# Low parts of weights on VectorE in two halves, bias tiles kept beside the keys, transpositions four steps behind the scores

## The chip, the cores and the metric

The kernel runs on one core of a Trainium2 chip. Five engines of that core work in parallel, each through its own queue in order: TensorE (PE in the profile, with its weight loads as PEld), VectorE (DVE), ScalarE (ACT), GpSimd (POOL) and SyncE (SP), which here issues nearly all DMAs. An instruction waits at the head of its queue until what it needs is there, and everything behind it on that engine waits too.

The metric is the device time of one execution in microseconds (us), as the median of three runs. The profile is of one further execution.

## The reference, cut to what matters

One layer of a streaming encoder. The tokens (1024 of a new stream, 64 of a running one) are normalized and projected to ten groups of columns; two kinds of attention follow, then gates, two projections, a merge and an output projection. The parts around the change:

```python
def stick_breaking(q, k, v, q_pos, k_pos):                # branch A ("sb"), 8 heads of 64
    z = jnp.einsum("bqhd,bkhd->bhqk", q, k).astype(jnp.float32) * ATTN_SCALE
    causal = k_pos[None, :] < q_pos[:, None]
    log_beta = jax.nn.log_sigmoid(z)
    log_keep = jnp.where(causal, jax.nn.log_sigmoid(-z), 0.0)
    suffix = lax.cumsum(log_keep, axis=3, reverse=True) - log_keep
    w = jnp.where(causal, jnp.exp(log_beta + suffix), 0.0)
    return jnp.einsum("bhqk,bkhd->bqhd", w.astype(v.dtype), v)

def band_attention(q, k, v, q_pos, k_pos, rel_bias):      # branch B ("cb"), 8 heads of 64
    s = jnp.einsum("...qhd,...khd->...hqk", q, k).astype(jnp.float32) * ATTN_SCALE
    rel = jnp.clip(q_pos[..., :, None] - k_pos[..., None, :], -REL_CLIP, REL_CLIP) + REL_CLIP
    bias = jnp.moveaxis(rel_bias[:, rel], 0, -3).astype(jnp.float32)
    s = jnp.where(mask, s + bias, NEG_INF)
    p = jax.nn.softmax(s, axis=-1).astype(v.dtype)
    return jnp.einsum("...hqk,...khd->...qhd", p, v)

...
    b_sb = (o_sb.reshape(lead + (WIDTH_SB,)) * jax.nn.silu(z_sb)) @ w_proj_sb
    b_cb = (o_cb.reshape(lead + (WIDTH_CB,)) * jax.nn.silu(z_cb)) @ w_proj_cb
    h = jax.nn.sigmoid(g_sb) * b_sb + jax.nn.sigmoid(g_cb) * b_cb
    return x + h @ w_out
```

## The kernel before, in words

**Precision.** Products of weights and activations run on operands of type fp32r. Each operand is split into a high part (a copy to that type on ScalarE) and a low part (what the copy lost, a subtraction), and three products are added: high by high, high by low, low by high. In class `Weights`, `hi` is the copy (L115) and `lo` the subtraction (L122), on GpSimd unless an engine is named; `split` issues both.

**Stages.** The input projection (L464, then L634) takes the first half. The attention loop at the end of the listing below (`for i in range(len(seq) + LAG)`) runs from about 512 to 872 us of the span. The projection of the "cb" branch (L925) and the output projection (L1419) follow.

**The attention loop.** `seq` lists 136 steps: branch "sb" first, then "cb"; in each, four pairs `p` of heads; in each pair the 64 running tokens (`t == 8`, both heads in one step), then eight blocks `t` of 128 queries for each head `hd`. A step of "sb" is as wide as `(t + 1) * 128` keys, one of "cb" at most 640. Iteration `i` issues, in this order:

- `mid(i - 2, 1)`: for "cb", reciprocal and scaling on VectorE (L1060, L1061); `mid(i - 1, 0)`: for "sb", the scan that forms the suffix products and the multiplication (L1057, L1058, VectorE), for "cb" the exponential (L1054, ScalarE)
- `tr(i - LAG)`: transpositions of the finished weights `be` on TensorE (L1088) in groups of up to four blocks into `pt`, of which there are two buffers in PSUM, and copies from there to `wT` on ScalarE (L1095)
- half of the step's filler (`fill`)
- `qk(i)`: scores `z` on TensorE (L1034, three buffers); for "sb" two sigmoids on ScalarE (L1036 into `kp`, L1037 into `be`) and, ahead of these, a one-column memset of `kp` on GpSimd (L1023); for "cb" one custom VectorE instruction that adds the bias tile and keeps a running minimum (L1039)
- loads: `load_z`, and in `prefetch` the next queries, keys, values and bias tiles, each at its own `t`
- stores that were put off (`flush`), the rest of the filler, and, after each second block of queries, the products with the values `av` (L1123), whose result VectorE multiplies by the gate (L1127)

`be` has four buffers, `kp` three.

**The filler.** `fill(n)` pulls `n` matmuls out of the generator `run_fill`: eight units of the input projection that were left over (72 matmuls each, L781), and then the "sb" output projection `proj_sb` (24 matmuls for each of 12 pieces, L881). They give TensorE work while VectorE and ScalarE finish a step. The eighth unit may not begin before step ("cb", 0, 1); until then what is asked of `fill` is owed. How much a step gets is in proportion to its width, out of `n_sb` for all "sb" steps and `n_cb = 72 + FP` for all "cb" steps. Whenever a unit or a piece `ci == 1` begins, the generator also splits the weights of the next one; inside `proj_sb`'s first stretch and the eighth unit, `og_step` splits the attention outputs (`og_hi` on ScalarE, `og_lo` on GpSimd for even pairs and VectorE for odd).

**The bias tiles.** `load_bias(p)` issues four DMAs and four memsets. The tiles live in pool `ay`, which is opened when "cb" begins, in the memory that the "sb" pool `axs` (with `kp`) has just left; the first pair's tiles are therefore loaded in the first iteration of "cb" (L1206), the later ones in the pair before, at `t == 4` (L1152).

```python
    FP = 180
    n_sb = 72 * (len(units) - 3)
    n_cb = 72 + FP
...
    LAG = 3
...
            if (b, p, t) == ("cb", 0, 8):
                sbx.close()
                yst = ExitStack()
                late["y"] = yst.enter_context(tc.tile_pool(name="ay", bufs=2))
                load_bias(0)
            qk(i)
```

## Time and profile before

| what | value |
|---|---|
| median of three runs | 1027.22 us (1025.51 to 1031.51) |
| the profiled execution | 1026.61 us, of which the span 1024.8 us |
| VectorE busy over the span | 630.6 us (62%) |
| ScalarE busy | 498.2 us (49%) |
| GpSimd busy | 340.7 us (33%) |
| granted TensorE clock, mean | 0.99 |

The page counts a matmul as busy until its modelled end, and matmuls overlap, so a share of 95% or more on PE means only that it hardly waited; the idle time in front of an instruction, and what ended it, says where it did. In groups of instructions, the number behind the second bar is the engine's idle time just before them, followed by what ended it. In the timeline a row is start, length, engine, line, operation, output <- inputs, shapes, count, and in brackets the idle time before it.

### The profile page before, as it was taken

Reading aid. Unit: us, or ns where it says so; the run is one execution under the profiler, and the core shown is the slowest. Engines: PE = TensorE matmul, PEld = TensorE weight load, DVE = VectorE, ACT = ScalarE, POOL = GpSimd, SP = SyncE. Lnnn points to the kernel's source line nnn. Section 1 sums busy time; section 2 is a strip of 40 time slices with the busy share of each in tenths; the row PEclk is TensorE's granted clock in tenths of the full one; section 3 lists DMA queues with packets and bytes.
Section 4 is the critical chain, followed back from the end, with each engine's and each line's share of the span. In section 5 each row is a group of like instructions: output and inputs, shape, how many; then the busy total and the mean of one; then the engine's idle time right before and its main releaser. Section 6 shows DMA issues by size and latency. Waiting matters only on the chain.

```text
span 1024.8 us, 20492 instructions
## 1 busy us (share of the span) xinstructions
PE 973.2 (95%) x7568; PEld 922.4 (90%) x7568; DVE 630.6 (62%) x1181; ACT 498.2 (49%) x1149; POOL 340.7 (33%) x356
## 2 busy tenths in 40 slices
PE   6999999999999999999989999996989988999998
PEld 5999999998989999999978978885877777999998
DVE  5466673984534555422078879893776765389735
ACT  6544442444343333333267867773765654366320
POOL 3377662124444444542210011012110100377451
PEclk9999999999999999999999999998999998999999
DMA  7636468435555333332686657646898871773542
GB/s 244 205 124 208 164 236 290 127 106 160 165 170 153 96 95 125 111 97 81 183 223 177 162 136 183 157 127 177 226 249 244 229 219 45 230 237 102 191 133 87
DMA packets 177412, 171.04 MB, mean 167 GB/s; under 512 B 35040, under 2 KB 163168, under 8 KB 177184
## 3 DMA queue, kind: packets, MB, share of 16 engines
q1 hardware_dynamic: 168592, 161.41, 53.3%
q10 hardware_dynamic: 8720, 8.33, 2.5%
q8 instruction: 60, 0.98, 0.4%
q14 instruction: 40, 0.33, 0.1%
HBM read 110.96 MB, written 58.72 MB: 166 GB/s over the span
## 4 chain that ended last, share of the span: by engine, by line
PE 77%; DMA 7%; DVE 5%; SPq 4%; ACT 3%; issue 2%; POOL 1%; DVEq 0%; ACTq 0%; POOLq 0%
PE b L634 23%; PE acc L464 19%; PE b L1419 7%; PE o L1123 7%; PE acc L781 6%; PE pt L1088 5%; PE z L1034 5%; PE b L925 2%; SPq L51 2%; PE acc L881 1%; DVE be L1039 1%; DVE be L1061 1%; DMA d_ksbT<-hl 1%; DMA wo<-in_w_out_dram 1%; PE pk L349 1%
## 5 line engine op out<-in xcount | busy, mean ns | idle before, releaser
L1088 PE MATMUL pt<-ident,be 128*128 128x128 f32 (+1 forms) x568 | 88.7, 281 | 29.4 <-ACT wT L1095 12.2
L1095 ACT ACTIVATE wT<-pt 128x512 f32<-128x512 f32 (+3 forms) x200 | 87.5, 474 | 58.8 <-PE pt L1088 58.4
L122 POOL TENSOR_TENSOR wlo<-wraw,whi 128x1024 fp32r<-128x1024 f32 x22 | 53.5, 2433 | 176.9 <-ACT whi L115 131.9
L1088 PEld LDWEIGHTS pt<-ident,be 128*128 128x128 f32 (+1 forms) x568 | 65.6, 142 | 44.0 <-issue 17.9
L1057 DVE TENSOR_TENSOR_SCAN kp<-kp,imp 128x128 f32<-128x128 f32 (+7 forms) x64 | 88.0, 1375 | 0.0
L1034 PE MATMUL z<-ks,sq 128*128 128x320 f32 (+5 forms) x384 | 85.0, 330 | 0.0
L464 PE MATMUL acc<-whi,xa 128*128 128x256 f32 x256 | 74.2, 292 | 0.0
L1123 PE MATMUL o<-wT,vp 128*64 128x256 f32 (+1 forms) x608 | 70.7, 369 | 1.0 <-ACT wT L1095 1.0
L464 PE MATMUL acc<-wlox,xm 128*128 128x256 f32 x256 | 70.8, 278 | 0.0
L464 PE MATMUL acc<-whi,xm 128*128 128x256 f32 x256 | 70.8, 278 | 0.0
L464 PE MATMUL acc<-wlo,xa 128*128 128x256 f32 x256 | 70.7, 278 | 0.0
L464 PE MATMUL acc<-whix,xb 128*128 128x256 f32 x256 | 70.6, 278 | 0.0
L464 PE MATMUL acc<-whix,xm 128*128 128x256 f32 x256 | 70.6, 278 | 0.0
L1054 ACT ACTIVATE be<-be,sm 128x640 f32<-128x640 f32 (+5 forms) x68 | 47.6, 701 | 46.4 <-DVE sm L1039 41.5
L1123 PEld LDWEIGHTS o<-wT,vp 128*64 128x64 f32 x608 | 44.6, 142 | 26.5 <-issue 7.0
L1034 PEld LDWEIGHTS z<-ks,sq 128*128 128x128 f32 x384 | 66.0, 191 | 0.9
L781 PE MATMUL acc<-xm,whi 128*128 128x384 f32 (+1 forms) x192 | 65.7, 342 | 0.0
L1058 DVE TENSOR_TENSOR be<-be,kp 128x128 f32<-128x128 f32 (+8 forms) x68 | 57.3, 843 | 9.1
L642 DVE TENSOR_TENSOR u<-b,s 128x256 f32<-128x256 f32 (+1 forms) x48 | 21.0, 439 | 63.6 <-PE b L634 63.3
L1036 ACT ACTIVATE kp<-z 128x384 f32<-128x384 f32 (+6 forms) x104 | 52.1, 501 | 8.2 <-PE z L1034 6.6
L1037 ACT ACTIVATE be<-z 128x384 f32<-128x384 f32 (+6 forms) x104 | 52.6, 505 | 0.0
L1127 DVE TENSOR_TENSOR zt<-o,zt 128x256 f32<-128x256 f32 (+1 forms) x40 | 15.3, 383 | 54.1 <-PE o L1123 47.4
(297 smaller groups left out, 3133.0 us busy)
## 6 DMA issues: line engine op xcount, KB each, us to landing
wraw<-in_w_in_dram SPq DMA_DIRECT2D x32, 512.0 KB, 4.5
wrawx<-in_w_in_dram SPq DMA_DIRECT2D x16, 512.0 KB, 4.5
sq<-d_qsbT SPq DMA_DIRECT2D x32, 192.0 KB, 3.6
sq<-d_qcbT SPq DMA_DIRECT2D x32, 192.0 KB, 4.1
gt<-d_gsb SPq DMA_DIRECT2D x30, 192.0 KB, 3.3
xt<-in_x_prompt_dram SPq DMA_DIRECT2D x8, 512.0 KB, 5.0
d_kcbT<-hl SPq DMA_DIRECT2D x8, 512.0 KB, 4.5
d_qcbT<-hl SPq DMA_DIRECT2D x8, 512.0 KB, 5.7
```

What stands on the lines that cost most here:

```text
L122: (eng or G).tensor_tensor(out=l, in0=raw, in1=h[:].bitcast(F32), op=OP.subtract)
L464: TE.matmul(ps, x, w, start=m == 0, stop=m == len(steps) - 1)
L634: TE.matmul(ps[:, :m], w[:, hl_, k], right[s](x)[:, k, a:b], start=s < 3 and k == 0 and e == 0, stop=k == 3 and e == 2, skip_group_check=s ...
L781: TE.matmul(ps[:, :b - a], w[:, k], xk(x, k)[:, a:b], start=k == 0 and n == 0, stop=k == KT - 1 and n == 2)
L1034: TE.matmul(z[:r, :m], s[:, c, q0:q0 + r], ks[:, h, o + x:o + y], start=e == 0, stop=e == len(parts) - 1)
L1037: A.activation(be[:r, x:y], z[:r, :m], AF.Sigmoid, scale=0.125)
L1057: V.tensor_tensor_scan(kp[:r, n - 1::-1], kp[:r, n - 1::-1], im[:, ::-1], 0.0, op0=OP.mult, op1=OP.add)
L1058: V.tensor_tensor(out=be[:r, :n], in0=be[:r, :n], in1=kp[:r, 1:n + 1], op=OP.mult)
L1088: TE.transpose(pt[:kr, x, :r], be[:r, kb * 128:kb * 128 + kr], ident[:r, :r])
L1095: A.activation(w[:, sl:sl + m, q0:q0 + r], pt[:, :m, :r], AF.Copy)
L1123: TE.matmul(o[hd * 64:hd * 64 + 64, c0:c1], vv[:kr, kb, hd * 64:hd * 64 + 64], (wT[b, p, j, hd, s // 4][:kr, s % 4, c0:c1] if j < 4 else w ...
L1419: TE.matmul(ps[:, t], left[s](xs_, k)[:, ts_], wt_[:, k], start=s < 3 and t == k == e == 0, stop=k == 3 and e == 2, skip_group_check=s > 2 ...
```

## The change

Five edits, all in the attention and what it draws on.

1. A new generator `halves` in `Weights`. The filler calls it four times, six matmuls of a unit (three of a projection piece) apart: the first call issues the high copy on ScalarE, the third and the fourth each half of the low subtraction, now on VectorE. The two splits that were issued at `ci == 1` use it.
2. `og_lo` of the "sb" branch runs on VectorE for all pairs.
3. The bias tiles are allocated in pool `am`, beside the queries and values; the first "cb" pair's are loaded in the last "sb" pair at `t == 4`.
4. `LAG` is 4: `tr(i - 4)` and what hangs on it.
5. `FP` is 132, 48 less, and each of the four iterations behind the last step asks for 12 filler matmuls, where it asked for none.

```diff
+        def halves(self, key):
+            self.hi(key)
+            yield
+            raw, pool, shape, extra = self.raw.pop(key)
+            h = self.sp[key][0]
+            l = pool.tile(shape, F32R, name="wlo" + extra, bufs=2)
+            m = shape[1] // 2
+            for c in (slice(0, m), slice(m, 2 * m)):
+                yield
+                V.tensor_tensor(out=l[:, c], in0=raw[:, c], in1=h[:, c].bitcast(F32), op=OP.subtract)
+            self.sp[key] = (h, l)
...
+    cut = [None]
...
-                            W.split(("u", j + 1) if j + 1 < len(units) else ("p", 0))
+                            cut[0] = W.halves(("u", j + 1) if j + 1 < len(units) else ("p", 0))
+                        if ci == 1 and n == 0 and k % 2 == 0:
+                            next(cut[0], None)
...
-        (V if p % 2 else G).tensor_tensor(out=og(b, 1, p)[:, a:e], in0=ot[:, :e - a],
+        (G if b == "cb" and p % 2 == 0 else V).tensor_tensor(out=og(b, 1, p)[:, a:e], in0=ot[:, :e - a],
...
-                W.split(("p", i + 1))
+                cut[0] = W.halves(("p", i + 1))
...
+                        if ci == 1 and uu == 0 and m == 0:
+                            next(cut[0], None)
...
-        if b == "cb" and t == 4:
+        if (b == "cb" or p == NPAIR - 1) and t == 4:
             load_bias(np_)
...
-        bt = late["y"].tile([128, 576], F32, name="bias8", bufs=1)
+        bt = am.tile([128, 576], F32, name="bias8", bufs=1)
...
-            bt = late["y"].tile([128, 640], F32, name="bias", bufs=4)
+            bt = am.tile([128, 640], F32, name="bias", bufs=4)
...
-    FP = 180
+    FP = 132
...
-    LAG = 3
+    LAG = 4
...
+        else:
+            m = 12
...
-                load_bias(0)
```

The places where it moves instructions, as each engine's queue has them. First TensorE where "sb" ends and "cb" begins: `kss` are the first "cb" scores, `be` the weights that are transposed. Before:

```order
L1088 MATMUL pt_9045<-ident_129,be_8924 128x128 x4
L1088 MATMUL pt_9052<-ident_129,be_8924 128x128 x3
L1034 MATMUL z_9074<-kss_8684,sqs_6521 128x288 x4
L1034 MATMUL z_9080<-kss_8684,sqs_6521 128x288 x4
L1088 MATMUL pt_9096<-ident_129,be_8962 128x128 x4
L1088 MATMUL pt_9102<-ident_129,be_8962 128x128 x4
L1034 MATMUL z_9110<-ks_8638,sq0_8897 128x128 x2
L1088 MATMUL pt_9122<-ident_129,be_9021 128x128 x4
L1088 MATMUL pt_9128<-ident_129,be_9021 128x128 x4
L1034 MATMUL z_9136<-ks_8638,sq0_8897 128x128 x2
```

And now:

```order
L1105 MATMUL pt_9049<-ident_129,be_8889 128x128 x4
L1105 MATMUL pt_9056<-ident_129,be_8889 128x128 x3
L1051 MATMUL z_9067<-kss_8686,sqs_6521 128x288 x4
L1051 MATMUL z_9073<-kss_8686,sqs_6521 128x288 x4
L1105 MATMUL pt_9091<-ident_129,be_8932 128x128 x4
L1105 MATMUL pt_9098<-ident_129,be_8932 128x128 x3
L1051 MATMUL z_9105<-ks_8639,sq0_8902 128x128 x2
L1105 MATMUL pt_9117<-ident_129,be_8970 128x128 x4
L1105 MATMUL pt_9123<-ident_129,be_8970 128x128 x4
L1051 MATMUL z_9131<-ks_8639,sq0_8902 128x128 x2
L1105 MATMUL pt_9138<-ident_129,be_9012 128x128 x4
L1105 MATMUL pt_9144<-ident_129,be_9012 128x128 x4
```

The last "sb" step (eight blocks, `be_9021` before and `be_9012` now) is transposed one score later, and one "sb" step more stands behind the first "cb" scores.

Second, SyncE around the last "sb" pair, where `kss` are the keys of the first "cb" step and `bias` the tiles of the first "cb" pair. Before, the bias loads stand alone at the end:

```order
L734 DMA vp<-d_cbv 128x8x128
L735 DMA vs<-in_cache_cb_v_dram 128x4x128
L736 DMA vs<-d_cbv 64x128
L694 DMA d_osb_112<-zt 128x256
L1159 DMA bias_9061<-d_rb_117 64x576
L1159 DMA bias_9061<-d_rb_118 64x576
L1163 DMA bias<-d_rb_117 128x640
L1163 DMA bias<-d_rb_118 128x640
L1101 DMA zt<-d_zcb_89 128x64
```

Now they stand between the key loads and the weights of the projection:

```order
L51 DMA kss<-d_ccbT_81 64x512 x4
L51 DMA kss<-d_kcbT_73 64x64 x4
L706 DMA d_gcb_106<-sg 128x288
L706 DMA d_gcb_106<-sg 128x32
L1176 DMA bias_8748<-d_rb_117 64x576
L1176 DMA bias_8748<-d_rb_118 64x576
L1180 DMA bias<-d_rb_117 128x640
L1180 DMA bias<-d_rb_118 128x640
L706 DMA d_osb_112<-zt 128x256
L109 DMA wraw<-in_w_proj_sb_dram 128x4x256
```

They come some twenty queue entries earlier. On GpSimd their four memsets follow: they stand ahead of the `kp` memsets of the last seven "sb" steps.

Third, VectorE in the third "sb" pair, where one split's two halves now stand among scans (`SCALAR_TENSOR_TENSOR`) and multiplications; before there was none of them here, and one whole `wlo` of 128x1024 on GpSimd:

```order
L138 TENSOR_TENSOR wlo_7817<-wraw_7356,whi_7797 128x512
L1074 SCALAR_TENSOR_TENSOR kp_7870<-kp_7870,ims_6517 128x576
L1075 TENSOR_TENSOR be_7869<-be_7869,kp_7870 128x576
L1074 SCALAR_TENSOR_TENSOR kp_7913<-kp_7913,imp_6514 128x128
L1075 TENSOR_TENSOR be_7912<-be_7912,kp_7913 128x128
L138 TENSOR_TENSOR wlo_7817<-wraw_7356,whi_7797 128x512
```

The loop issues 12 such pairs of halves in all: two ahead of the first scan, eight between scans and "cb" steps, one behind the last step, one after the loop.

## Prediction

> **What bounds the kernel now.** I first read the busy shares, then the groups of instructions with their idle time, then windows of the attention, and last the timeline around each wait.

> ```profile
> PE 973.2 (95%) x7568; PEld 922.4 (90%) x7568; DVE 630.6 (62%) x1181; ACT 498.2 (49%) x1149; POOL 340.7 (33%) x356
> ```

> TensorE is busy for 973 of 1024.8 us, so a change can gain only where TensorE stands, or where it runs slowly. Among the groups one stands out by its idle time, the transpositions in the attention:

> ```profile
> L1088 PE MATMUL pt<-ident,be 128*128 128x128 f32 (+1 forms) x568 | 88.7, 281 | 29.4 <-ACT wT L1095 12.2 <-DVE be L1061 10.9 <-DVE be L1058 5.3
> ```

> TensorE stood 29.4 us in front of them: 12.2 for ScalarE's copies that empty `pt`, 16.2 (10.9 + 5.3) for VectorE to finish `be`. That is most of what TensorE waits for at all, and the change aims at nothing else. How near the other engines are shows in windows: a "sb" pair, two "cb" pairs, the tail of the loop, and the matmuls behind it (behind the times: length, then busy time of PE, PEld, DVE, ACT, POOL, then granted clock).

> ```profile
> 599.00:644.00 45.00, 43.33 (x326) 37.90 (x326) 39.41 (x41) 33.51 (x85) 4.22 (x19) 1.00 0.58 149
> ...
> 743.00:783.00 40.00, 36.66 (x283) 30.98 (x282) 30.61 (x102) 24.48 (x64) 4.04 (x6) 1.00 0.86 237
> 783.00:823.00 40.00, 36.14 (x276) 30.09 (x275) 27.25 (x96) 22.82 (x62) 2.97 (x5) 1.00 0.87 241
> ...
> 863.00:872.00 9.00, 7.04 (x46) 4.91 (x46) 2.91 (x9) 3.87 (x10) 0.00 (x0) 0.81 0.04 15
> 872.00:893.00 21.00, 19.69 (x121) 18.88 (x118) 8.03 (x14) 6.39 (x12) 7.50 (x6) 1.00 0.76 233
> ```

> VectorE is second everywhere: 39.4 of 45 us in "sb", 27 to 31 of 40 in "cb". There is some room for more on it, not much.

> **Low parts off GpSimd.** The GpSimd subtractions of the attention that come just ahead of a TensorE wait, and two VectorE multiplications of the same shape, 128x512:

> ```profile
> 526.51 2.73 POOL L122 TENSOR_TENSOR wlo<-wraw,whi 128x1024 fp32r<-128x1024 f32 x1 [4.73 <-ACT whi L115]
> ...
> 712.41 2.38 POOL L122 TENSOR_TENSOR wlo<-wraw,whi 128x1024 fp32r<-128x1024 f32 x1 [15.32 <-issue]
> 754.33 2.35 POOL L122 TENSOR_TENSOR wlo<-wraw,whi 128x1024 fp32r<-128x1024 f32 x1 [8.06 <-ACT whi L115]
> 799.16 2.38 POOL L122 TENSOR_TENSOR wlo<-wraw,whi 128x1024 fp32r<-128x1024 f32 x1 [22.32 <-ACT whi L115]
> 843.61 2.36 POOL L122 TENSOR_TENSOR wlo<-wraw,whi 128x1024 fp32r<-128x1024 f32 x1 [28.77 <-ACT whi L115]
> ```
> ```profile
> 527.20 2.59 DVE L1058 TENSOR_TENSOR be<-be,kp 128x512 f32<-128x512 f32 x1
> ...
> 661.95 0.69 DVE L1058 TENSOR_TENSOR be<-be,kp 128x512 f32<-128x512 f32 x1
> ```

> The one that starts inside a GpSimd subtraction takes 2.59 us, the other 0.69: VectorE lost 1.9 us until GpSimd was done (526.51 + 2.73 = 529.24; the multiplication ends at 529.79). TensorE then waits:

> ```profile
> 529.93 0.76 PE L1088 MATMUL pt<-ident,be 128*128 128x128 f32 x4 [1.85 <-DVE be L1058]
> ...
> 716.35 0.41 PE L1088 MATMUL pt<-ident,be 128*128 128x128 f32 x2 [2.46 <-DVE be L1061]
> ...
> 756.97 0.41 PE L1088 MATMUL pt<-ident,be 128*128 128x128 f32 x2 [2.23 <-DVE be L1061]
> ...
> 801.91 0.52 PE L1088 MATMUL pt<-ident,be 128*128 128x128 f32 x3 [1.27 <-DVE be L1061]
> ...
> 846.40 0.63 PE L1088 MATMUL pt<-ident,be 128*128 128x128 f32 x4 [1.85 <-DVE be L1061]
> ```

> Each stands two to four us behind the start of one of those five subtractions; together 9.66 us. With none left on GpSimd in the loop I take back **9.0**, between 5 (the new halves delay some of the same weights) and 9.7.

> [...]

> Two of these waits are followed by a stretch of half clock:

> ```profile
> 530.30:533.70 3.40, 3.40 (x15) 3.30 (x14) 3.13 (x4) 2.02 (x5) 0.10 (x1) 0.50 0.44 104
> 694.10:700.90 6.80, 3.27 (x16) 2.78 (x18) 2.18 (x10) 3.87 (x10) 0.58 (x4) 0.50 1.03 281
> 847.80:851.10 3.30, 3.30 (x15) 2.62 (x15) 1.66 (x6) 1.98 (x5) 0.00 (x0) 0.50 0.00 0
> 868.30:871.60 3.30, 3.30 (x15) 1.88 (x17) 0.00 (x0) 0.57 (x2) 0.00 (x0) 0.50 0.00 0
> ```

> TensorE was busy throughout 530.3 to 533.7 and 847.8 to 851.1 at clock 0.50, so half of 6.7 us is lost; with the waits gone I take **3.3** back (0 to 3.3).

> What VectorE pays: of twelve pairs of halves, eight stand between scans and "cb" steps, 16 x 0.69 = 11.0 us; six `og_lo` of at most 128x384 come from GpSimd, below 6 x 0.69 = 4.1. In return nine GpSimd subtractions no longer stretch it, by up to 1.9 us each, 17 in all. Net about nothing on VectorE, which has 5.6 us of room in the "sb" pair and more in "cb"; on TensorE's path I put it at 0 (bounds: 2 us less, 15 us more if nothing comes back). Behind a half in VectorE's queue stand the next scan or bias addition; they wait at most for ScalarE's high copy, issued 12 filler matmuls earlier.

> **Four steps behind.** A transposition now waits for weights that are one step older. Apart from the five waits above, 16.2 - 9.66 = 6.5 us of waiting on VectorE are left. The wait goes where VectorE is late by less than a step, and shrinks where it is later; I take **4.5** (bounds 0 and 6.5). `be` has four buffers, so its writer follows the transpositions of the same iteration; the scores stand behind these on TensorE anyway, and the write waits for the scores, so nothing is added. What may come late next is `pt`: two buffers, emptied by copies that stand behind an exponential on ScalarE. Of the 12.2 us there, all but those at the boundary and in the tail (below) stay in the sum.

> **Bias tiles early.** The boundary between the branches:

> ```profile
> 689.73 1.22 DVE L1058 TENSOR_TENSOR be<-be,kp 128x1024 f32<-128x1024 f32 x1
> 690.98 1.11 SPq L1159 DMA_DIRECT2D bias<-d_rb  x2
> ...
> 695.05 0.46 DVE L1039 CUSTOM_DVE_ANT_0 be<-z,bias 128x288 f32<-128x288 f32 x1 [4.10 <-DMA bias<-d_rb]
> ...
> 697.62 1.97 PE L1088 MATMUL pt<-ident,be 128*128 128x128 f32 x8 [7.90 <-ACT wT L1095]
> ```

> The load is issued when the last multiplication of "sb" leaves `kp` (690.95), and the first bias addition waits 4.10 us for it. TensorE waits 7.90 for copies that stand behind the exponential, which waits for that addition. With the tile there, the addition still follows the multiplication on VectorE, so the chain shortens by **4.1** and TensorE keeps 3.8 of its 7.9. Bounds 3 and 5.8: above 4.1 only if the half clock behind it (3.27 us busy at 0.50 in 694.1 to 700.9, 1.6 lost) went too, which I do not count.

> [...]

> The four loads move past some twenty entries of SyncE's queue, to just behind these key loads:

> ```profile
> 660.87 2.88 SPq L51 DMA_DIRECT2D kss<-d_kcbT  x4
> ```

> So they start at about 665, and if they land as after 690.98 (4.1 us for the first, more for the others) the tiles are there near 670. Their memsets hold GpSimd until then, with the `kp` memset of the next step behind them, which this multiplication needs:

> ```profile
> 668.49 2.73 DVE L1058 TENSOR_TENSOR be<-be,kp 128x640 f32<-128x640 f32 x1
> ```

> It would start some 2 us late; today it is stretched by as much by a GpSimd subtraction. I put 0 (bounds 0 and 2).

> **Filler into the tail.** 48 matmuls at 19.69 / 121 = 0.16 us leave the "cb" steps and fill the four last iterations: 7.8 us each way. What they cover there:

> ```profile
> 866.40 0.77 PE L1088 MATMUL pt<-ident,be 128*128 128x128 f32 x5 [1.60 <-ACT wT L1095]
> 867.53 0.76 PE L1088 MATMUL pt<-ident,be 128*128 128x128 f32 x5 [0.36 <-ACT wT L1095]
> ```

> 1.96 us of waiting, and the half clock from 868.3 (3.3 busy, 1.65 lost): **3.6** back. Whether "cb" gets shorter by all of 7.8 is open: VectorE has 31 us of work in a pair of 40, and once the waits above and two us of filler per pair are gone, a pair comes down to about 35, with VectorE near 32. I take 4.8 of the 7.8, that is **3.0** lost (0 to 7.8).

> **The sum.** 9.0 + 3.3 + 4.5 + 4.1 + 3.6 - 3.0 = 21.5. The profiled execution took 1026.61 (span 1024.8 and 1.8 around it), which gives 1005.1; its median of runs lies 0.6 higher. Forecast **1005 us**.

> **The rivals.**

> - *The wait changes its name.* The copies into `wT` stand behind the exponential on ScalarE and `pt` has two buffers, so TensorE stops one group later. For it: 12.2 us already wait there. Against it: 10.2 of these have a cause of their own (bias, tail). It would give 5 of the 9.66, 1.7 of the clock, none of the 4.5, and the rest: 5 + 1.7 + 4.1 + 3.6 - 3 = 11.4, so 1016.
> - *All of it comes back.* 9.7 + 3.3 + 6.5 + 5.8 + 3.6 and the other 2.3 us of the copies' 12.2, nothing lost in "cb": 31.2, so 996. For it: the waits are all in front of one group, and the older weights cover several at once. Against: VectorE near 32 of 35.
> - *VectorE becomes the bound*, on the slow side. The 15 us of new instructions land on VectorE and the stretched time does not come back, because those instructions were waiting for something else. Price: 15 us on the path from 515 to 863, less 4.1 and 3.6: 7.3 slower, 1034. It decides once VectorE's work in a pair passes TensorE's: 39.4 + 2 x 0.69 against 43.3 in "sb", 30.6 + 1.4 + 1 against some 35 in "cb". Both are below, and the 2.59 beside 0.69 speaks against it. [...]
> - *The early load does not help*: it lands no sooner because SyncE reaches it late, or holds the `kp` memsets for longer than a step. Without the 4.1 and with 2 more: 1011, inside the range.

> **How the numbers follow.** Forecast 0.56 (1000 to 1011), the wait with another name 0.24, all back 0.12, VectorE the bound 0.04, early load of no use 0.04. The range of 994 to 1017 takes in all but the slow rival, the upper third of the second case and the ends of the costs. A measurement of this kernel tells about 0.5%, or 5.1 us, from no change; faster by more than that are the first, third and fifth case and nearly all of the second: 0.93. Within it 0.04, slower 0.03.

> **What would show it.** In the profile after, the transpositions' idle time should fall from 29.4 to below 12, with nearly nothing left for VectorE; no multiplication of 128x512 should take over 1 us; the first bias addition should follow the last multiplication with no idle time, and TensorE's wait there should be near 4; the half clock at about 530, 848 and 868 should be gone. The halves should take 0.7 us. I am wrong if the copies' 12.2 grow, if VectorE shows 95% or more in "cb" pairs that are still 38 us long, or if scans begin to wait for GpSimd.

## The result, and the profile after

| kernel | median | runs | ratio to before, 95% interval |
|---|---|---|---|
| before | 1027.53 us | 4, 1025.51 to 1031.51 | |
| after | 1012.54 us | 4, 1009.8 to 1016.43 | 0.9857 [0.983, 0.9883] |
| before, later group | 1023.98 us | 17, 1020.93 to 1031.24 | |
| after, later group | 1009.22 us | 6, 1007.85 to 1010.64 | 0.9841 [0.9811, 0.9871] |

The kernel is 15 us faster, where 21.5 were forecast. The profiled execution took 1009.8 us (span 1008.0), 16.8 less than that of before; it is the fastest of its four runs. In code of after, line numbers are 12 to 18 higher: L1088 is now L1105, L1095 L1112, L1123 L1140, L1039 L1056, L1058 L1075.

The busy shares of after, then the groups of transpositions and value products (behind the second bar: idle time ahead of them, and what ended it), with the value products of before between them:

```profile
PE 970.5 (96%) x7568; PEld 920.6 (91%) x7568; DVE 633.2 (63%) x1211; ACT 498.3 (49%) x1149; POOL 307.3 (30%) x338
```
```profile
L1105 PE MATMUL pt<-ident,be 128*128 128x128 f32 (+1 forms) x568 | 89.3, 282 | 11.7 <-ACT wT L1112 10.7 <-DVE be L1075 0.8
L1140 PE MATMUL o<-wT,vp 128*64 128x256 f32 (+1 forms) x608 | 71.0, 357 | 3.7 <-ACT wT L1112 3.5
```
```profile
L1123 PE MATMUL o<-wT,vp 128*64 128x256 f32 (+1 forms) x608 | 70.7, 369 | 1.0 <-ACT wT L1095 1.0
```

The transpositions' 29.4 us of idle time became 11.7. Of the 16.2 that VectorE ended, 0.8 is left. What ScalarE's copies end grew: without the boundary and the tail it was 12.2 + 1.0 - 7.90 - 1.96 = 3.3 us and is 10.7 + 3.5 - 6.37 = 7.8. VectorE's stretched multiplications are gone, and a half of a low part takes what was assumed:

```profile
L1075 DVE TENSOR_TENSOR be<-be,kp 128x512 f32<-128x512 f32 x8 | 5.5, 692 | 1.1
L138 DVE TENSOR_TENSOR wlo<-wraw,whi 128x512 fp32r<-128x512 f32 x24 | 15.9, 685 | 12.6 <-ACT whi L115 12.6
```

The attention loop in windows cut where the running tokens' scores of a pair begin (stretch, length, busy time of PE, PEld, DVE, ACT, POOL, granted clock, DMA share, GB/s): the first "sb" pair, the four "cb" pairs, the tail to the last value product, and the sum over all nine. Before:

```profile
512.49:555.75 43.26, 39.82 (x276) 35.41 (x276) 35.02 (x37) 31.13 (x78) 4.19 (x17) 0.96 0.75 198
...
687.20:743.32 56.12, 44.24 (x318) 37.89 (x317) 30.95 (x96) 30.56 (x75) 8.61 (x14) 0.94 0.66 185
743.32:782.66 39.34, 36.00 (x277) 30.32 (x277) 29.95 (x102) 24.14 (x64) 4.04 (x6) 1.00 0.85 237
782.66:822.92 40.26, 36.40 (x277) 30.35 (x277) 27.54 (x96) 23.09 (x61) 2.97 (x5) 1.00 0.87 241
822.92:863.21 40.29, 36.18 (x265) 31.05 (x264) 27.07 (x92) 22.79 (x60) 2.36 (x1) 0.96 0.52 149
863.21:872.48 9.27, 7.30 (x48) 5.01 (x46) 2.70 (x9) 3.73 (x10) 0.00 (x0) 0.82 0.04 14
sum 359.99, PE 329.04 PEld 282.90 DVE 266.50 ACT 236.16 POOL 36.19; mean PE 36.56 PEld 31.43 DVE 29.61 ACT 26.24 POOL 4.02
```

After:

```profile
512.49:550.67 38.18, 37.34 (x269) 33.24 (x269) 34.16 (x39) 30.13 (x76) 1.58 (x16) 1.00 0.86 223
...
681.04:732.60 51.56, 42.94 (x308) 36.61 (x307) 33.57 (x104) 30.38 (x74) 0.58 (x4) 0.93 0.60 169
732.60:770.30 37.70, 35.75 (x266) 29.73 (x265) 28.39 (x102) 24.51 (x65) 0.58 (x4) 1.00 0.85 231
770.30:807.00 36.70, 34.74 (x267) 29.27 (x266) 26.24 (x97) 23.36 (x62) 0.94 (x4) 1.00 0.84 231
807.00:840.15 33.15, 30.72 (x229) 25.75 (x229) 24.24 (x90) 20.19 (x55) 0.00 (x0) 1.00 0.65 185
840.15:856.24 16.09, 16.09 (x124) 14.04 (x123) 6.87 (x17) 6.17 (x15) 0.00 (x0) 1.00 0.39 117
sum 343.75, PE 327.62 PEld 281.86 DVE 263.64 ACT 236.13 POOL 9.02; mean PE 36.40 PEld 31.32 DVE 29.29 ACT 26.24 POOL 1.00
```

The loop is 16.2 us shorter, which is the whole difference of the two profiled executions but for 0.6. The first pair gives 5.1, the other "sb" pairs together 1.1, the "cb" pairs 4.6, 1.6, 3.6 and 7.1; the tail takes 6.8 back (48 filler matmuls and a step more of transpositions and products: 124 matmuls where there were 48). The clock of 0.96 in the first and the last full pair is now 1.00.

One place did not go as forecast, the boundary. A timeline of after (start, length, engine, line, what; in brackets the idle time before it): GpSimd's memsets of the new bias tiles and of `kp`, VectorE's multiplication behind them, the first bias addition, and TensorE's wait; then the window of TensorE's half clock there.

```profile
664.15 0.14 POOL L1181 MEMSET bias<- 64x64 f32 x1 [9.59 <-DMA bias<-d_rb]
...
665.38 0.18 POOL L1040 MEMSET kp<- 128x1 f32 x3
```
```profile
665.52 0.83 DVE L1075 TENSOR_TENSOR be<-be,kp 128x640 f32<-128x640 f32 x1 [3.11 <-POOL kp L1040]
...
687.09 0.45 DVE L1056 CUSTOM_DVE_ANT_0 be<-z,bias 128x288 f32<-128x288 f32 x1
```
```profile
689.66 1.97 PE L1105 MATMUL pt<-ident,be 128*128 128x128 f32 x8 [6.37 <-ACT wT L1112]
```
```profile
687.13:693.96 6.83, 4.30 (x20) 4.15 (x20) 2.50 (x13) 4.65 (x12) 0.00 (x0) 0.50 0.16 46
```

The bias addition follows at once, as meant; the 4.10 us of waiting for the load are gone. But GpSimd stood 9.59 us for that load with three `kp` memsets queued behind, and VectorE stood 3.11 us for these. So VectorE reaches the boundary late, and TensorE waits 6.37 us where 3.8 were forecast.

### The profile page after: what moved, and what is told of

Same layout as the page of the kernel before. It is cut to its first block, busy times and chain, and to the rows that moved or that the text cites. A ratio compares the mean times of both kernels' runs of the same rounds, so it can differ in the third digit from the quotient of the medians.

```text
span 1008.0 us, 20461 instructions
## 1 busy us (share of the span) xinstructions
PE 970.5 (96%) x7568; PEld 920.6 (91%) x7568; DVE 633.2 (63%) x1211; ACT 498.3 (49%) x1149; POOL 307.3 (30%) x338
## 4 chain that ended last, share of the span: by engine, by line
PE 84%; DVE 5%; ACT 4%; issue 3%; DMA 3%; SPq 1%; POOL 0%; DVEq 0%; ACTq 0%
PE b L646 23%; PE acc L476 19%; PE acc L794 8%; PE b L1437 8%; PE o L1140 7%; PE pt L1105 6%; PE z L1051 5%; PE b L942 4%; PE acc L896 2%; DVE be L1056 2%; ACT wT L1112 1%; ACT be L1071 1%; DMA d_ksbT<-hl 1%; PE pk L361 1%; DMA wrawx<-in_w_in_dram 1%
## 5 line engine op out<-in xcount | busy, mean ns | idle before, releaser
L1112 ACT ACTIVATE wT<-pt 128x512 f32<-128x512 f32 (+3 forms) x200 | 87.7, 475 | 54.8 <-PE pt L1105 54.2
L1105 PE MATMUL pt<-ident,be 128*128 128x128 f32 (+1 forms) x568 | 89.3, 282 | 11.7 <-ACT wT L1112 10.7
L1105 PEld LDWEIGHTS pt<-ident,be 128*128 128x128 f32 (+1 forms) x568 | 66.8, 143 | 24.0 <-ACT wT L1112 14.7
L1140 PE MATMUL o<-wT,vp 128*64 128x256 f32 (+1 forms) x608 | 71.0, 357 | 3.7 <-ACT wT L1112 3.5
L1140 PEld LDWEIGHTS o<-wT,vp 128*64 128x64 f32 x608 | 43.6, 136 | 30.4 <-ACT wT L1112 8.7
L1075 DVE TENSOR_TENSOR be<-be,kp 128x128 f32<-128x128 f32 (+8 forms) x68 | 51.6, 759 | 12.0 <-POOL kp L1040 3.1
L1040 POOL MEMSET kp<- 128x1 f32 x68 | 6.5, 99 | 165.8 <-DVE be L1075 165.7
L476 PEld LDWEIGHTS acc<-whi,xa 128*128 128x128 f32 x256 | 47.9, 188 | 0.1
```

The lines of the kernel that those rows point to most:

```text
L476: TE.matmul(ps, x, w, start=m == 0, stop=m == len(steps) - 1)
L1105: TE.transpose(pt[:kr, x, :r], be[:r, kb * 128:kb * 128 + kr], ident[:r, :r])
L1112: A.activation(w[:, sl:sl + m, q0:q0 + r], pt[:, :m, :r], AF.Copy)
L1140: TE.matmul(o[hd * 64:hd * 64 + 64, c0:c1], vv[:kr, kb, hd * 64:hd * 64 + 64], (wT[b, p, j, hd, s // 4][:kr, s % 4, c0:c1] if j < 4 else w ...
```

## The experiments

Within a group the runs of before are shared.

| run | median | ratio to before, 95% interval |
|---|---|---|
| split_on_gpsimd | 1011.44 us | 0.9865 [0.9846, 0.9884] |
| lag3 | 1012.15 us | 0.9879 [0.9857, 0.9901] |
| bias_at_boundary | 1010.99 us | 0.9865 [0.9844, 0.9886] |
| fill_in_loop | 1011.09 us | 0.9868 [0.9847, 0.989] |
| lag4_alone | 1014.79 us | 0.9894 [0.9869, 0.9918] |
| halves_alone | 1016.94 us | 0.9905 [0.9879, 0.993] |
| both_undone | 1019.12 us | 0.9938 [0.9915, 0.9962] |
| edges_later | 1008.82 us | 0.9841 [0.9814, 0.9869] |
| after_again | 1009.22 us | 0.9841 [0.9811, 0.9871] |
| edges_again | 1007.03 us | 0.982 [0.979, 0.9851] |
| edges_lag5 | 1022.03 us | 0.9957 [0.9936, 0.9979] |
| edges_wide | 1005.09 us | 0.9818 [0.9781, 0.9854] |

### Each part undone by itself

The low parts whole on GpSimd again:

```diff
-                cut[0] = W.halves(("p", i + 1))
+                W.split(("p", i + 1))
+                cut[0] = iter(())
```

> The changed kernel, but the low parts of the weights in the attention are again one whole 128x1024 subtraction on GpSimd; four steps behind, early bias tiles and filler in the tail stay. The prediction's terms (lock waits 9.0, half clock at 530 and 848 3.3) say 12.3 us slower than the changed kernel's 1012.5, about 1025; a multiplication of 128x512 takes over 2 us again where it meets such a subtraction, and the half clock near 530 or 848 comes back. Rival: with the fourth step TensorE has enough lead over VectorE to hide a stall of 2 us, so the move of the low parts was worth little once the other was there: 1012 to 1016, with multiplications of over 2 us in the profile, but hardly any TensorE wait behind them.

Three steps behind again:

```diff
-    LAG = 4
+    LAG = 3
...
-            m = 12
+            m = 16
```

> The changed kernel with the transpositions three steps behind the scores instead of four (and 16 filler matmuls in each of three last iterations instead of 12 in four). The prediction's term says 4.5 us slower, about 1017, with TensorE's waits in front of the transpositions named VectorE again. Rival: the fourth step only gave the waits another name (ScalarE's copies), since VectorE sets the pace in the wide steps whatever the distance: within 1.5 us of 1012.5. A third: the fourth step is what hides most, 8 us or more slower, 1020 and up.

The first bias tiles loaded at the boundary, in the later pool:

```diff
-        if (b == "cb" or p == NPAIR - 1) and t == 4:
+        if b == "cb" and t == 4:
...
-            bt = am.tile([128, 640], F32, name="bias", bufs=4)
+            bt = late["y"].tile([128, 640], F32, name="bias", bufs=4)
...
+                load_bias(0)
```

> The changed kernel with the first pair's bias tiles loaded at the boundary between the branches again, in the pool of the branch behind it. The prediction's term says 4.1 us slower, about 1016.6. From the profile of the changed kernel I now think that the early load gave back about 3 us of it, since GpSimd's memsets of the tiles' edges wait for the load in front of the memsets of kp, and VectorE stood 3.11 us for those: 1 to 2 us slower, 1013.5 to 1014.5, no wait of VectorE for GpSimd of 3 us in the last 'sb' steps, and TensorE's wait at the boundary 7.5 to 8 us instead of 6.37.

The 48 filler matmuls back in the loop:

```diff
-    FP = 132
+    FP = 180
...
-            m = 12
+            m = 0
```

> The changed kernel with the 48 filler matmuls back in the 'cb' steps and none in the last iterations. The prediction's terms (3.6 back in the tail, 3.0 lost because 'cb' shortens by less than 7.8) say 0.6 us slower, 1013.1, with the half clock behind the loop back. Rival, VectorE paces the wide steps: taking filler out of 'cb' shortened it by at most 2 us, so putting it back costs 2, and the tail gets shorter by 7.8 less the waits that come back (3.6): 2 us faster, about 1010.5. The other side, TensorE paces 'cb': 3.6 us slower, 1016.

None of the four costs anything that can be measured in the time; all intervals overlap that of after. So the 12.3 us by which the prediction priced the low parts are not lost when they go back, and the rival of that run is right. In split_on_gpsimd a multiplication that meets a GpSimd subtraction takes 2.32 us, where others of its shape take about 0.3, but VectorE ends only 1.5 us of the transpositions' idle time (L1077 and L1080 are multiplication and scaling there), and no half clock came back at 530 or 848 (granted clock 1.00 there):

```profile
556.63 2.32 DVE L1077 TENSOR_TENSOR be<-be,kp 128x128 f32<-128x128 f32 x1
```
```profile
L1107 PE MATMUL pt<-ident,be 128*128 128x128 f32 (+1 forms) x568 | 89.3, 283 | 12.8 <-ACT wT L1114 11.1 <-DVE be L1077 0.8 <-DVE be L1080 0.7
```

A smaller cost stays possible. In the profiled executions the loop is 3.5 us longer in split_on_gpsimd (347.3) and 3.7 in lag3 (347.4) than in after (343.8); these two executions took 1012.57 and 1016.05 us where the medians of their kernels are 1011.44 and 1012.15, and a cost of this size lies inside the intervals.

Of lag3 the interval leaves 0 to about 4.5 us against after's 0.9857; its profiled execution (1016.05 us) shows what three steps do when the bias load is late:

```profile
669.66 0.15 POOL L1181 MEMSET bias<- 64x64 f32 x1 [10.89 <-DMA bias<-d_rb]
```
```profile
672.55 0.83 DVE L1075 TENSOR_TENSOR be<-be,kp 128x640 f32<-128x640 f32 x1 [5.92 <-POOL kp L1040]
```
```profile
673.52 0.74 PE L1105 MATMUL pt<-ident,be 128*128 128x128 f32 x5 [2.98 <-DVE be L1075]
```

VectorE stands 5.92 us for `kp`, and 2.98 of it reach TensorE. With four steps the 3.11 us of after reached TensorE only at the boundary: its first wait behind 665.52 is the one of 6.37 us at 689.66.

In bias_at_boundary the addition waits for the load again:

```profile
687.30 0.46 DVE L1056 CUSTOM_DVE_ANT_0 be<-z,bias 128x288 f32<-128x288 f32 x1 [3.77 <-DMA bias<-d_rb]
```

These 3.77 us against the 3.11 of after: the early load changed one wait for another of nearly the same length. TensorE's wait at the boundary is 7.46 us here, about the 7.5 to 8 expected, against 6.37 in after. So the early load is worth some 1.1 us at this place, less than the times can show.

In fill_in_loop, the "cb" pairs and the tail:

```profile
681.63:735.30 53.67, 45.19 (x320) 39.11 (x319) 35.45 (x107) 31.43 (x76) 0.59 (x4) 0.94 0.60 173
735.30:773.52 38.22, 36.40 (x277) 31.98 (x277) 27.95 (x101) 23.84 (x64) 0.58 (x4) 1.00 0.85 236
773.52:811.66 38.14, 36.66 (x277) 31.89 (x277) 27.54 (x99) 23.16 (x62) 0.87 (x4) 1.00 0.89 243
811.66:845.85 34.19, 32.48 (x241) 28.27 (x240) 25.34 (x92) 21.19 (x56) 0.00 (x0) 1.00 0.64 181
845.85:856.51 10.66, 9.08 (x77) 6.35 (x75) 2.96 (x10) 5.16 (x14) 0.00 (x0) 1.00 0.04 14
```

The four pairs take 164.2 us against 159.1 in after, the tail 10.66 against 16.09. Taking 48 matmuls out of "cb" gives 5.1 there and costs 5.4 in the tail: nothing. The half clock behind the loop came back in this run, as was expected:

```profile
867.20:868.90 1.70, 1.70 (x7) 1.70 (x6) 0.77 (x2) 0.00 (x0) 0.00 (x0) 0.50 0.91 280
```

The span behind the loop is 1.0 us longer than in after (152.8 against 151.8), but in after_again, the same kernel as after, it is 150.4, so this is within its spread.

### Each part by itself, and both undone

If undoing either costs nothing, the two parts may be doing the same work. lag4_alone is the kernel before with one number changed:

```diff
-    LAG = 3
+    LAG = 4
```

> The kernel before with one number changed: transpositions four steps behind the scores. Low parts on GpSimd, bias tiles loaded at the boundary and filler in the loop stay as before. Undoing each part of the change by itself cost nothing that could be measured (1011.0 to 1012.2). Theory now: the fourth step and the halves on VectorE are substitutes, each hides or removes the same stalls, so this one edit by itself brings most of the gain: ratio 0.987 to 0.990, about 1012.5 to 1016. Rival: no part matters by itself and the gain needs both of them (or comes from the bias tiles and the filler): ratio 0.995 or more. The prediction's own term for it was 4.5 us: ratio 0.9955.

halves_alone is the kernel before with `halves` and `og_lo` as in after, and nothing else of the change:

```diff
-                W.split(("p", i + 1))
+                cut[0] = W.halves(("p", i + 1))
...
-        (V if p % 2 else G).tensor_tensor(out=og(b, 1, p)[:, a:e], in0=ot[:, :e - a],
+        (G if b == "cb" and p % 2 == 0 else V).tensor_tensor(out=og(b, 1, p)[:, a:e], in0=ot[:, :e - a],
```

> The kernel before with only the low parts in two halves on VectorE (and og_lo of 'sb' there); transpositions three steps behind, bias tiles at the boundary, filler in the loop. The prediction's terms: 9.0 + 3.3 = 12.3 us faster, ratio 0.988, 1013.5. The theory of substitutes gives about the same, 0.987 to 0.990. Rival: the gain came from the other parts, ratio 0.995 or more.

both_undone is split_on_gpsimd and lag3 together; `og_lo` of "sb" stays on VectorE, as in split_on_gpsimd:

```diff
-                cut[0] = W.halves(("p", i + 1))
+                W.split(("p", i + 1))
+                cut[0] = iter(())
...
-    LAG = 4
+    LAG = 3
...
-            m = 12
+            m = 16
```

> The changed kernel with the low parts whole on GpSimd again and the transpositions three steps behind again; early bias tiles and filler in the tail stay. Theory of substitutes: neither undone alone cost anything, both together bring nearly all of it back: ratio 0.995 to 1.000, 1021 to 1026, with VectorE waits of about 2 us each behind the GpSimd subtractions and half clock near 530 and 850. Rival, the two are worth little, and the gain is in the bias tiles and the filler (7.7 us by the prediction 4.1 + 3.6): ratio 0.987 to 0.992.

Alone, the fourth step brings 10.9 us (1025.26 x 0.0106), the halves 9.7, and what is left when both are gone 6.4: 27 in sum, where the change with all of them brings 15. So they are substitutes in large part; each of the three has an interval of about 2.5 us on either side, far less than the 12 us by which the sum exceeds the whole. Both undone lost 8 to 10 us against after (0.9938 against 0.9857 and 0.9841), a little less than the theory's 0.995 to 1.000, and the half clock that was expected near 530 and 850 did not come (granted clock 1.00 there).

The 6.4 us that are left are not explained by the runs. In the profiled execution of both_undone (1022.32 us, median 1019.12), the "cb" pairs and the tail take 175.3 us against 185.3 before and the first "sb" pair 2.2 less, but the last "sb" pair takes 6.4 more (49.4 against 43.1), where GpSimd waits 10.22 us for the early bias load. Which of the early tiles, the filler and `og_lo` shortens "cb" there, no run separates.

The transpositions' idle time in lag4_alone, in halves_alone (L1075 multiplies, L1078 scales) and in both_undone (L1077 and L1080):

```profile
L1088 PE MATMUL pt<-ident,be 128*128 128x128 f32 (+1 forms) x568 | 89.3, 283 | 15.1 <-ACT wT L1095 12.7 <-DVE be L1061 1.1 <-DVE be L1058 0.8
```
```profile
L1105 PE MATMUL pt<-ident,be 128*128 128x128 f32 (+1 forms) x568 | 89.5, 283 | 19.8 <-ACT wT L1112 12.3 <-DVE be L1078 4.0 <-DVE be L1075 2.4
```
```profile
L1107 PE MATMUL pt<-ident,be 128*128 128x128 f32 (+1 forms) x568 | 89.8, 283 | 22.0 <-DVE be L1077 8.4 <-ACT wT L1114 7.0 <-DVE be L1080 5.3
```

The fourth step by itself takes VectorE's 16.2 us down to 1.9, although every low part of the weights is still on GpSimd and a subtraction there still stretches VectorE's work. A timeline of lag4_alone, a scan and one that meets a GpSimd subtraction, and the transposition that follows:

```profile
523.65 1.22 DVE L1057 TENSOR_TENSOR_SCAN kp<-kp,imp 128x512 f32<-128x512 f32 x1
...
525.95 3.10 DVE L1057 TENSOR_TENSOR_SCAN kp<-kp,imp 128x512 f32<-128x512 f32 x1
```
```profile
525.13 2.84 POOL L122 TENSOR_TENSOR wlo<-wraw,whi 128x1024 fp32r<-128x1024 f32 x1 [4.36 <-ACT whi L115]
```
```profile
528.94 0.60 PE L1088 MATMUL pt<-ident,be 128*128 128x128 f32 x4
```

The scan takes 3.10 us instead of 1.22, and the transpositions at 528.94 have no idle time before them, where TensorE stood 1.85 us in the kernel before. By these rows the extra step is more lead than the stall is long. The stall itself is still there (3.10 us against 1.22 for the same scan); with three steps TensorE stood 1.85 us behind such a stall, with four not at all, so here the lead set what it cost.

### The memsets off the path

If the early load lost its 3 us to GpSimd's queue, moving four memsets must bring them:

```diff
+    edges = []
+
+    def set_edges():
+        for bt in edges:
+            G.memset(bt[0:64, 576:640], BIG)
+            G.memset(bt[64:128, 0:64], BIG)
+        edges.clear()
...
-            G.memset(bt[0:64, 576:640], BIG)
-            G.memset(bt[64:128, 0:64], BIG)
             BI[h] = bt
+            edges.append(bt)
+            if p:
+                set_edges()
...
+                set_edges()
             qk(i)
```

> The changed kernel, with the memsets of the first pair's bias tiles' edges on GpSimd moved from the early load to the first 'cb' step, so that no memset of kp stands behind them. In the profile of the changed kernel GpSimd waited there 9.59 us for the load and VectorE 3.11 us for a memset of kp; in that of the variant with three steps the load landed later and GpSimd waited 10.89. Theory: VectorE leaves 'sb' about 3 us earlier, TensorE's wait at the boundary falls from 6.37 to about 3.3, 2 to 3.5 us faster than the changed kernel: ratio 0.982 to 0.9845. Rival: VectorE is paced by TensorE there and catches up anyway, TensorE's wait stays at 6 or the exponential becomes late for another reason: ratio 0.985 to 0.987.

It was run again beside the changed kernel:

> The changed kernel once more, beside its variants of this group. Expected: ratio 0.986 as before (0.9857 and the variants with one part undone 0.9865 to 0.9879). If the difference to the variant with later edge memsets is the 2 to 3 us of the boundary, that one stands 0.002 to 0.003 lower in the same group; if it was chance, they agree.

> The variant with the first pair's edge memsets in the first 'cb' step once more. Expected 0.9835 to 0.9845; theory: its boundary wait on TensorE (3.6 us in its first profile) is fixed by the chain from VectorE's last multiplication, and no longer by when the load lands, so it is about 3.6 again. Rival: the first profile caught an early load; the wait is 6 or more and the ratio 0.986.

The boundary in edges_again, with the memsets, the first bias addition and TensorE:

```profile
673.86 0.14 POOL L1175 MEMSET bias<- 64x64 f32 x1
```
```profile
684.31 0.45 DVE L1056 CUSTOM_DVE_ANT_0 be<-z,bias 128x288 f32<-128x288 f32 x1
```
```profile
686.88 1.09 PE L1105 MATMUL pt<-ident,be 128*128 128x128 f32 x8 [3.60 <-ACT wT L1112]
```

GpSimd no longer waits for the load, VectorE arrives 2.8 us earlier than in after (684.31 against 687.09), and TensorE waits 3.60 us (3.60 in both profiles of this kernel). The "cb" pair that begins at the boundary takes 48.50 us in edges_again, where it takes 51.56 in after, and the half clock behind the wait lasts 3.4 us instead of 6.8 (mean clock 0.96 instead of 0.93):

```profile
681.03:729.53 48.50, 42.58 (x309) 35.82 (x307) 30.95 (x101) 30.25 (x74) 0.80 (x4) 0.96 0.63 180
```

The median is 2.2 us below that of the changed kernel in the same group. edges_later has a ratio of 0.9841, lower than the first 0.9857 of after and the same as that of after_again, which came out lower than the 0.986 expected. The intervals of the ratios overlap, so the times alone don't prove it; the rows show the mechanism and its size.

### One step more, and more filler in the wide steps

```diff
-        be = am.tile([128, NP], F32, name="be", bufs=4)
+        be = am.tile([128, NP], F32, name="be", bufs=5)
...
-    LAG = 4
+    LAG = 5
...
-            m = 12
+            m = 10
```

> The variant with later edge memsets, with the transpositions five steps behind the scores and five buffers for be (10 filler matmuls in each of five last iterations). Theory: with four steps TensorE's waits for VectorE are already gone (0.8 us of one wait left at 515), and what is left in 'cb' are waits for ScalarE's copies of the same step, which no distance helps: within 1.5 us of the variant with four. Rival: the distance still pays, as from three to four (2 us or more faster). On the other side: the weights that wait longer hold up nothing, but a longer drain at the end costs 1 to 2 us.

Neither theory nor rival: 15 us slower than with four. TensorE's waits for weights are the lowest of all (7.0 us in front of the transpositions), but it waits for queries. TensorE in edges_lag5, then SyncE's waits between 740 and 770 us (in total, times, longest), then the load of these queries there and in edges_again:

```profile
767.79 1.39 PE L1051 MATMUL z<-kss,sqs 128*128 128x288 f32 x8 [2.10 <-DMA sqs<-d_qcbT]
...
810.31 2.17 PE L1051 MATMUL z<-kss,sqs 128*128 128x288 f32 x8 [3.89 <-DMA sqs<-d_qcbT]
```
```profile
SPq L1118 <- DMA d_ocb<-zt: 6.1, 2, 3.8
```
```profile
763.42 2.47 SPq L51 DMA_DIRECT2D sqs<-d_qcbT  x4
```
```profile
756.73 2.48 SPq L51 DMA_DIRECT2D sqs<-d_qcbT  x4
```

`zt`, the tile of the gate and then of the output, has three buffers. With the products one step later its store is later too, SyncE's next loads into it wait 6.1 us for stores, and keys and queries queue behind that: issued 6.7 us later in the span. That the order on SyncE is the cause is read from the rows; no run moved those loads. The two waits for queries (6.0 us) and the half clock that follows each (3.4 us each by the mean clocks: 0.84 in 764 to 772, 0.93 in 772 to 778, and 0.79 in 808 to 816; at clock 0.50 that costs an estimated 3.4 us together) make up 9.4 of the 10.6 us between the two profiled executions. The medians are 15 us apart; what adds the rest, no trace shows.

The last run changes how "cb" 's filler is spread:

```diff
-    wt = {"sb": lambda n: n, "cb": lambda n: n + 150}
+    wt = {"sb": lambda n: n, "cb": lambda n: max(0, n - 200)}
```

> The variant with later edge memsets, with more of 'cb' 's filler in the wide steps (weight n - 200, none below 200, instead of n + 150): some 6 matmuls or 1.0 us of a pair move there from the narrow steps. Theory, VectorE sets the pace in the wide steps (it runs there without a pause) and TensorE in the narrow ones: the narrow steps get shorter by 1.0 us per pair, the wide ones by less longer, 2 to 4 us faster in all. Rival: TensorE is as full in the wide steps (waits of 0.2 to 0.9 us only), so they get longer by as much: within 1 us; or the narrow steps, whose chain of exponential, scaling and copies is then bare, stall: slower by 2 or more.

The second and third "cb" pair of edges_wide:

```profile
727.28:765.07 37.79, 35.40 (x266) 30.50 (x265) 28.61 (x102) 24.86 (x66) 0.58 (x4) 1.00 0.81 229
765.07:802.44 37.37, 34.94 (x267) 30.12 (x266) 26.14 (x97) 23.20 (x62) 0.90 (x4) 1.00 0.87 240
```

They are not shorter than the 37.69 and 36.69 of edges_again, the same kernel without this edit. The whole loop takes 341.25 us against 341.67, so the rival, "within 1 us", is right. The median is 1.9 us below edges_again, inside the interval, and 2.8 of the 3.2 us between the two profiled executions lie ahead of the loop and behind it. This speaks against the idea that VectorE alone sets the pace in the wide steps; what does is left open.

## Why the prediction was right, and by how much it was off

The direction, the place and four of the five signs in the profile were as said: half clock at 530, 848 and 868 is gone (after has none in the loop but at the boundary), the stretched multiplications are gone, the halves take 0.69 us, and the transpositions wait 11.7 us, below 12. The fifth came by half: the first bias addition follows without idle time, but TensorE's wait there is 6.37 us, not near 4. Two of the signs of being wrong came close: the copies' waits outside boundary and tail grew (3.3 to 7.8), and VectorE began to wait for GpSimd, at a multiplication and not at a scan.

The size was 21.5, against 16.8 between the profiled executions and 15.0 and 14.8 between the medians. The range held both medians, but the point of 1005 was 4 to 8 us too low, and the first group's 1012.54 lies nearer to the 1016 of the rival "the wait changes its name". Two terms were too large, and a third a little.

- **Low parts and four steps, 9.0 + 4.5.** VectorE's share of the waits went nearly to nothing, more than the 13.5 taken. But 4.5 us came back under ScalarE's name (3.3 to 7.8), so 16.2 + 3.3 - 0.8 - 0.3 (now ahead of scores) - 7.8 = 10.6 us are left: 2.9 too many. The rival "the wait changes its name" was priced as a case of its own; it came true for less than half of the waits it was about, beside the forecast. The step that failed here is the split of the 13.5 into two terms that each depend on their own edit: the 9.0 for the low parts do not hang on moving them, since four steps hide those stalls (in lag4_alone VectorE ends 1.9 us of the transpositions' waits, 16.2 in the kernel before) and undoing the move costs nothing that can be measured (split_on_gpsimd). The sum came near all the same because both terms were taken out of the same 16.2 us of waiting.
- **Half clock, 3.3.** The clock of both pairs concerned went from 0.96 to 1.00. The size is right. It does not hang on the low parts either: the first pair's clock is 1.00 in lag4_alone and in halves_alone alike.
- **Bias tiles, 4.1.** The step that failed is "I put 0 (bounds 0 and 2)" for the memsets that hold GpSimd. The load held them 9.59 us, and VectorE stood 3.11. TensorE's wait fell by 1.5 us (7.90 to 6.37), which is 2.6 too few. With the memsets elsewhere the wait is 3.60, close to the 3.8 of the prediction.
- **Filler, 3.6 in the tail and 3.0 lost.** In "cb" 5.1 of the 7.8 us came back, where 4.8 were taken; in the tail 7.8 - 5.4 = 2.4 came back, where 3.6 were taken. Together that is 0.3 us lost inside the loop instead of 0.6 won, 0.9 too many.
- **VectorE as the bound** did not come: its busy time in the loop fell (266.5 to 263.6 us in the sums) though it had more to do, because it is no longer stretched: in split_on_gpsimd, where the halves are gone from it and the stretching is back, it is 266.1.

21.5 - 2.9 - 2.6 - 0.9 = 15.1, where the loop is 16.2 shorter in the profiled executions. These are sums over rows of two executions, not prices of the edits: the runs show that the edits' prices do not add.

Two readings of the prediction are off without consequence. The copies' waits at the boundary and in the tail are 7.90 + 1.96 = 9.9 us, not 10.2, and in the window of the tail ScalarE (3.87 us) comes second and not VectorE (2.91).

The variant with the memsets moved has lower medians than both kernels (1008.82 and 1007.03 us, ratios 0.9841 and 0.982), with intervals that overlap those of after.

## What to carry to other kernels

Price two remedies for one wait together: removing what stalls an engine and giving its reader more lead are substitutes here, and each by itself shows about two thirds of the gain (10.9 and 9.7 of 15 us). A load that is issued earlier also moves everything that its engine must do behind it (here GpSimd stood 9.59 us for it, and VectorE 3.11 us for GpSimd); ask which in-order queue then stands for the data, and who needs the next entry of that queue. More lead had an end here: with one step more, a buffer came free later, and TensorE stood 6.0 us for queries whose loads were queued behind it on SyncE.

## What was not expected of the hardware

How long TensorE stood did not by itself decide here whether half clock followed. Windows behind a wait of 2.46 us in the kernel before (the one at 716.35) and behind one of 2.39 us in both_undone:

```profile
716.50:719.90 3.40, 3.40 (x24) 2.74 (x24) 2.49 (x11) 2.83 (x8) 0.58 (x1) 1.00 0.80 214
```
```profile
719.54 0.66 PE L1107 MATMUL pt<-ident,be 128*128 128x128 f32 x2 [2.39 <-DVE be L1080]
```
```profile
719.60:723.00 3.40, 3.40 (x12) 3.21 (x13) 2.23 (x9) 2.37 (x7) 0.00 (x0) 0.52 0.88 227
```

The clock stayed at 1.00 behind the longer wait and fell to 0.52 behind the shorter. In the kernel before, half clock followed a wait of 1.85 us at 530.
